# Hybrid decoder trunk on one core: the dense part keeps the written order on TensorE, ScalarE and VectorE

## The chip, the core and the metric

The kernel runs on 1 core of a Trainium2 chip. Its time is the device time of one execution in microseconds; "before" was run three times, and one more execution was profiled. Five engines work side by side, each through its own queue and in the order of that queue: TensorE (PE in the profile, its weight loads PEld), VectorE (DVE), ScalarE (ACT), GpSimd (POOL) and SyncE (SP), which here only issues the loads of the weights.

## What is computed

Two decoder layers on 256 tokens of width 1024, all in float32. A layer is a mixer and a feed-forward part, each with RMSNorm before it and a residual add after it.

```python
def _mixer(h, w_in, b_in, conv_w, conv_b, conv_ln_g, conv_ln_b, sinks, w_out, b_out):
    z = jnp.einsum('bsd,de->bse', h, w_in) + b_in
    a, gate, q, k, v = jnp.split(z, SPLITS, axis=-1)
    conv_out = _conformer_conv(a, gate, conv_w, conv_b, conv_ln_g, conv_ln_b)
    attn_out = _swa_sink_attention(q, k, v, sinks)     # reshaped to heads
    y = jnp.concatenate([conv_out, attn_out], axis=-1)
    return jnp.einsum('bse,ed->bsd', y, w_out) + b_out

for l in range(DEPTH):
    x = x + _mixer(_rmsnorm(x, attn_norm[l]), ...)
    h = _rmsnorm(x, ffn_norm[l])
    x = x + (_swiglu(h, ...) if l % 2 == 0 else _moe(h, ...))
return _rmsnorm(x, final_norm)
```

The convolution gates `a` with `sigmoid(gate)`, runs 31 causal taps over 512 channels, normalises over the channels and applies swish. The attention has 8 query heads and 2 key heads of 64, a window of 128 and a learned sink per head. The dense feed-forward (layer 0) is 1024 to 2816 and back, the other (layer 1) picks two of eight experts of width 3584 for every token.

## The kernel before

Products are made from split operands: a float32 matrix is written as a high part (`wh`, rounded by ScalarE, line 190) and a low part (`wl`, the rest, by VectorE or POOL, line 191), and three matmuls (high x high, high x low, low x high) stand for one. A piece of a weight that is split at once is a granule (`Gran`). Its raw bytes come through a ring of 7 buffers, the split parts through 4.

Everything ahead of the experts is a list of steps. `drive` (line 212) goes through it: ahead of each step it writes the conversions of the granules up to three further on, then the step itself. So the written order of an engine is the order in which these Python calls are made. The list is `mixer(0)`, `ffn(0)`, `mixer(1)`, `moe_open`. Before the change the instructions that `drive` makes aren't held to that order: a planner puts each engine's instructions in a row when the program is built, by priority and by when it expects operands and buffers to be ready. `urgent` gives some steps a higher priority there. Only the first mixer's norm and transposes are called outside of `drive`. The experts' part (`run_experts`, with `route`) is in a block with `tc.manual_schedule` already, on the same three engines.

A mixer, for channels in four blocks `c` of 128 and tokens in two tiles `t`:

- `start`: statistics (lines 268 to 270), scaled rows `h`, 16 transposes into four PSUM banks (277), and `th`/`tl`, the high and low part of the transposed rows (289, 290). Two of the eight `k` share a bank.
- 14 input projections of 24 matmuls each (353): 4 for convolution blocks 0 and 1 (`ev_g`, line 411, a sigmoid; `ev_a`, line 418, the product `up`), 4 for q, 2 for k and v, and, written after `scores`, 4 for blocks 2 and 3. Two PSUM buffers `mm` take turns.
- the taps of the convolution are VectorE operations on PSUM (425, 430). They are handed out by `conv_piece(n)`, which writes the next n taps wherever it is called: 6 with each projection, some within the softmax and PV, 12 with each output-projection step. The first 8 taps of the last block are made by TensorE (`conv_pe`, line 404), from diagonal matrices that ScalarE writes (392), and from `uh`, `ul`, the parts of `up`.
- `scores`: v is transposed (489), then six groups of score matmuls (493, 495), each followed by `softmax`: reduction (515), sink (518, 520), exponentials on ScalarE (523, 525), sum (527), reciprocal (529), and POOL's normalisation (530). Between these it calls `conv_piece`.
- `pv`: six rounds of four transposes (547), one copy (549) and the matmul with v (550).
- the output projection (578): four granules for the attention half, with the first sums of LayerNorm in between (597, 617), then `ln_out`, then four granules for the convolution half; at the end the residual adds (302).

The two lines that set the order of VectorE in a softmax, and the loop of PV:

```python
            nc.vector.tensor_tensor(den, den, es, op=ALU.add)
            nc.vector.reciprocal(den, den)
```

```python
                        pT = work.tile([P, 512], F32, name="two")
                        nc.scalar.copy(pT, pp)
                        nc.tensor.matmul(po[s * HD:(s + 1) * HD, :], v[:, kb, s * HD:(s + 1) * HD], pT,
```

The dense feed-forward has 11 rounds of gate, up and down granules (matmuls on lines 695 and 720). Behind `mixer(1)` come `route` (771 to 844), which transposes `x` and picks the experts, and the experts' 384 weight pieces (matmuls on line 910).

Of the kernel before, what the change touches and what calls it, by code (L numbers as in the profile page):

```python
# [36 lines left out]
AHEAD = 3  # L37
# [8 lines left out]
def trunk_kernel(ctx: ExitStack, tc, x_in, attn_norm, ffn_norm, w_in, b_in, conv_w, conv_b,  # L46
# [165 lines left out]
    def drive(after):  # L212

        grans = [g for g, _ in steps if g is not None] + after
        nxt = 0
        done = 0
        for g, run in steps:
            if g is not None:
                done += 1
            while nxt < len(grans) and nxt < done + AHEAD:  # L220
                grans[nxt].conv()
                nxt += 1
            if g is not None:
                run(g.h, g.l)
            else:
                run()
        steps.clear()
# [913 lines left out]
    mixer(1)  # L1141
    add(moe_open)
    grans, run_experts = expert_steps(0)
    drive(grans[:AHEAD])
    run_experts()

    def finish():
# [45 lines left out]
```

## Time and profile before

| | us |
|---|---|
| median of 3 runs | 1369.43 |
| lowest, highest | 1368.93, 1371.05 |
| profiled execution | 1375.33 |
| its span, first to last instruction | 1373.6 |
| busy in the span: PE, DVE, ACT, POOL | 1300.9, 1161.1, 1016.1, 140.8 |
| DMA read from HBM | 413.35 MB |

All times below are microseconds from the start of the profiled span. A busy PE is not a PE at its peak: the ends of matmuls are modelled, and a matmul counts as busy at either level of its clock. A row of the timeline gives start, duration, engine, line, operation, out<-in, sizes and how many were merged; in brackets stands how long the engine had been idle, and what released it. The granted clock is a share of 2.4 GHz, mean over the stretch.

### The profile page before, as it was taken

The page shows a single profiled execution, that of the slowest core. Times are in us where ns is not written, and L with a number is a line of the kernel's source. Part 1 is how long each engine was busy: PE and PEld are TensorE (multiplying, and loading weights), DVE is VectorE, ACT ScalarE, POOL GpSimd, SP SyncE. Part 2 cuts the span into 40 slices and gives each one's busy share as a digit, 9 for nine tenths or more (in the row PEclk, how much of TensorE's full clock was granted, in tenths as well). Part 3 has the DMA queues.
Part 4 walks back from the last instruction along what each step waited for, and adds up shares of the span by engine and source line. Part 5 has one row for each costly group of instructions (what it writes and reads, how often), then busy time and mean ns, then how long its engine had stood idle before and what let it go on. Part 6 is the DMA issues. An engine that isn't in the chain of part 4 may idle for free. (4 is left out here: it accounts for less than half of the span.)

```text
span 1373.6 us, 18961 instructions
## 1 busy us (share of the span) xinstructions
PE 1300.9 (95%) x6939; PEld 1132.2 (82%) x6939; DVE 1161.1 (85%) x1142; ACT 1016.1 (74%) x1110; POOL 140.8 (10%) x97
## 2 busy tenths in 40 slices
PE   6998999998989799999999999999999999999986
PEld 6866999997867687778898889888889888888874
DVE  7785555557786899999989987999999999999985
ACT  5656444445644989899888787888987988888963
POOL 5551111115450000000000000000000000000000
PEclk9899999998898999999999999999999999999998
DMA  8823565564223899999999998999999999999991
GB/s 245 252 93 93 192 193 193 190 184 123 82 96 108 312 390 382 406 406 405 406 398 386 360 362 313 365 402 406 395 401 407 366 399 394 400 406 402 407 352 49
DMA packets 150178, 416.21 MB, mean 303 GB/s; under 512 B 8599, under 2 KB 49635, under 8 KB 150049
## 3 DMA queue, kind: packets, MB, share of 16 engines
q1 hardware_dynamic: 149760, 413.38, 81.2%
q8 instruction: 89, 1.46, 0.4%
q0 software_dynamic: 288, 1.05, 0.2%
q14 instruction: 41, 0.33, 0.1%
HBM read 413.35 MB, written 1.05 MB: 302 GB/s over the span
## 5 line engine op out<-in xcount | busy, mean ns | idle before, releaser
L191 DVE TENSOR_TENSOR wl<-raw,wh 128x1792 fp32r<-128x1792 f32 (+2 forms) x460 | 848.0, 1887 | 127.0 <-ACT wh L190 125.8
L190 ACT ACTIVATE wh<-raw 128x1792 fp32r<-128x1792 f32 (+2 forms) x496 | 758.9, 1554 | 263.9 <-PE pd L910 48.0
L910 PE MATMUL pu<-wh,xg 128*128 128x448 f32 x768 | 250.6, 372 | 6.3 <-DVE h L1029 6.3
L910 PE MATMUL pg<-wh,xg 128*128 128x448 f32 x768 | 247.0, 367 | 2.4 <-ACT h L1027 2.4
L910 PE MATMUL pd<-wh,g 128*128 128x512 f32 x672 | 239.3, 397 | 6.2 <-ACT wh L190 4.1
L910 PE MATMUL pu<-wl,xg 128*128 128x448 f32 x512 | 190.2, 371 | 6.6 <-DVE wl L191 6.6
L910 PE MATMUL pg<-wl,xg 128*128 128x448 f32 x512 | 189.6, 370 | 2.4 <-DVE wl L191 2.1
L910 PE MATMUL pd<-wl,g 128*128 128x512 f32 x448 | 179.8, 401 | 3.3 <-DVE wl L191 3.3
L910 PEld LDWEIGHTS pu<-wh,xg 128*128 128x128 f32 x768 | 146.9, 191 | 18.6 <-issue 7.6
L910 PEld LDWEIGHTS pg<-wh,xg 128*128 128x128 f32 x768 | 146.2, 190 | 14.8 <-ACT h L1027 3.0
L910 PEld LDWEIGHTS pd<-wh,g 128*128 128x128 f32 x672 | 130.6, 194 | 31.7 <-ACT wh L190 5.5
L910 PEld LDWEIGHTS pu<-wl,xg 128*128 128x128 f32 x512 | 98.8, 193 | 19.6 <-DVE wl L191 12.5
L910 PEld LDWEIGHTS pg<-wl,xg 128*128 128x128 f32 x512 | 98.2, 192 | 17.6 <-DVE wl L191 9.7
L910 PEld LDWEIGHTS pd<-wl,g 128*128 128x128 f32 x448 | 86.1, 192 | 26.2 <-DVE wl L191 10.1
L430 DVE SCALAR_TENSOR_TENSOR cv<-up,wcol,cv 128x256 f32<-128x256 f32 x226 | 98.4, 487 | 5.1 <-PE cv L404 3.1
L1150 POOL DMA_DIRECT2D h<-in_final_norm_dram x1 | 0.6, 599 | 910.6 <-PE pt L1087 910.6
L191 POOL TENSOR_TENSOR wl<-raw,wh 128x1024 fp32r<-128x1024 f32 x36 | 86.2, 2408 | 38.6 <-ACT wh L190 38.3
L353 PE MATMUL mm<-th,wh 128*128 128x256 f32 x224 | 65.9, 297 | 1.1 <-ACT sg L411 1.1
L353 PE MATMUL mm<-tl,wh 128*128 128x256 f32 x224 | 65.3, 293 | 1.0 <-DVE tl L290 1.0
L353 PE MATMUL mm<-th,wl 128*128 128x256 f32 x224 | 65.3, 293 | 0.9 <-POOL wl L191 0.7
L720 PE MATMUL acc<-wh,pp 128*128 128x512 f32 x176 | 50.3, 396 | 0.0
L695 PE MATMUL cv<-tl,wh 128*128 128x256 f32 x176 | 49.2, 280 | 0.3 <-DVE tl L290 0.3
(237 smaller groups left out, 1706.5 us busy)
## 6 DMA issues: line engine op xcount, KB each, us to landing
raw<-in_moe_w_gate_dram SPq DMA_DIRECT2D x128, 896.0 KB
raw<-in_moe_w_up_dram SPq DMA_DIRECT2D x128, 896.0 KB
raw<-in_moe_w_down_dram SPq DMA_DIRECT2D x96, 1024.0 KB
raw<-in_moe_w_down_dram SPq DMA_DIRECT2D x32, 512.0 KB
raw<-in_ffn_w_gate_dram SPq DMA_DIRECT2D x11, 1024.0 KB
raw<-in_ffn_w_up_dram SPq DMA_DIRECT2D x11, 1024.0 KB
raw<-in_ffn_w_down_dram SPq DMA_DIRECT2D x11, 1024.0 KB
raw<-in_w_in_dram SPq DMA_DIRECT2D x10, 1024.0 KB
```

Source lines behind the costliest of these rows:

```text
L190: nc.scalar.activation(self.h, src, AF.Copy)
L191: (lo or lo_eng()).tensor_sub(self.l, src, f32(self.h))
L353: nc.tensor.matmul(ps[:, :S], w(a, k), b[:, k, :], start=(n == 0), stop=(n == 3 * KD - 1))
L430: nc.vector.scalar_tensor_tensor(acc, up[:, c, k:k + S], w, acc, op0=ALU.mult, op1=ALU.add)
L695: nc.tensor.matmul(ps, a[:, k, :], b[:, k, :], start=(n_ == 0), stop=(n_ == 3 * KD - 1))
L720: nc.tensor.matmul(st["o"][t][cc], a[:, kk, tk], b[:, 0, cc * 512:(cc + 1) * 512], start=(first and i == 0), stop=(last and i == 2))
L910: nc.tensor.matmul(ps, a, b, start=(first and i == 0), stop=(last and i == len(mm) - 1))
L1150: nc.gpsimd.dma_start(fg, final_norm.unsqueeze(0).to_broadcast([P, D]))
```

## The change

The call that writes all steps of the dense part is put into a `tc.manual_schedule` block for TensorE, ScalarE and VectorE. Inside it these three engines run their instructions in the order in which the Python code makes them. SP and POOL aren't named and are still ordered by the planner. No instruction, tile or buffer count is changed.

```diff
     mixer(1)
     add(moe_open)
     grans, run_experts = expert_steps(0)
-    drive(grans[:AHEAD])
+    E = mybir.EngineType
+    with tc.manual_schedule(engines={E.PE, E.Activation, E.DVE}):
+        drive(grans[:AHEAD])
     run_experts()
```

## Rows read from the trace of the kernel before

**Rows 1.** Stretches; busy us (x instructions) of PE, PEld, DVE, ACT, POOL; clock, DMA share, GB/s.

```profile
45.40:71.70 26.30, 26.30 (x144) 19.78 (x144) 18.02 (x53) 19.72 (x57) 10.96 (x10) 0.81 0.72 222
71.70:81.10 9.40, 6.83 (x44) 6.26 (x44) 7.60 (x13) 6.11 (x16) 9.22 (x4) 0.82 0.36 112
81.10:105.10 24.00, 22.23 (x88) 14.21 (x88) 19.65 (x41) 9.86 (x17) 9.76 (x5) 1.00 0.28 88
133.60:312.50 178.90, 178.88 (x1269) 166.52 (x1267) 100.94 (x99) 80.71 (x90) 19.93 (x11) 1.00 0.57 183
378.40:410.70 32.30, 29.01 (x131) 20.64 (x130) 26.86 (x53) 15.84 (x32) 18.53 (x10) 0.95 0.31 102
444.40:1373.60 929.20, 887.97 (x4323) 774.80 (x4321) 865.11 (x606) 785.94 (x701) 2.01 (x3) 0.99 0.97 372
```

**Rows 2.** DVE in order of time: start us, us, operation, xcount, idle before.

```profile
47.63 0.69 DVE L515 TENSOR_REDUCE red<-acc 128x4 f32<-128x512 f32 x1 [1.72 <-PE acc L495]
...
50.07 0.68 DVE L515 TENSOR_REDUCE red<-acc 128x4 f32<-128x512 f32 x1
...
55.74 0.15 DVE L527 TENSOR_TENSOR red<-red 128x4 f32<-128x4 f32 x1
...
56.80 0.85 DVE L527 TENSOR_TENSOR red<-red 128x4 f32<-128x4 f32 x1
...
70.10 3.12 DVE L430 SCALAR_TENSOR_TENSOR cv<-up,wcol,cv 128x256 f32<-128x256 f32 x6
```

**Rows 3.** ACT in order of time, first mixer's attention.

```profile
51.99 0.37 ACT L523 ACTIVATE pp<-acc,red 128x128 f32<-128x128 f32 x1
...
53.37 0.21 ACT L525 ACTIVATE red<-red 128x4 f32<-128x4 f32 x1
...
65.50 0.47 ACT L523 ACTIVATE pp<-acc,red 128x256 f32<-128x256 f32 x1
...
66.42 0.20 ACT L525 ACTIVATE red<-red 128x2 f32<-128x2 f32 x1
...
67.50 2.01 ACT L190 ACTIVATE wh<-raw 128x1024 fp32r<-128x1024 f32 x2
...
70.83 0.48 ACT L411 ACTIVATE sg<-mm,vcol 128x256 f32<-128x256 f32 x1
```

**Rows 4.** PE in order of time, first mixer from its last projection on.

```profile
71.75 1.91 PE L547 MATMUL acc<-ident,pp 128*128 128x128 f32 x16
...
76.62 0.58 PE L404 MATMUL cv<-ul,h 128*128 128x256 f32 x1 [2.10 <-DVE ul L231]
...
83.27 2.82 PE L550 MATMUL mm<-two,v 128*64 128x512 f32 x6 [0.17 <-ACT two L549]
...
103.96 1.15 PE L617 MATMUL mm<-h,meanm 128*128 128x256 f32 x4 [1.28 <-DVE h L610]
```

**Rows 5.** Stretches of L353 (input projection) alone: busy us (x), clock.

```profile
32.00:45.00 13.00, 13.00 (x114) 13.00 (x113) 1.00 1.07 276
```

**Rows 6.** The same of L578 (output projection) alone.

```profile
92.00:97.00 5.00, 5.00 (x23) 3.85 (x21) 1.00 0.00 2
```

**Rows 7.** ACT in order of time, one copy between PE steps.

```profile
84.38 0.59 ACT L549 COPY two<-acc 128x512 f32<-128x512 f32 x1 [0.57 <-PE mm L550]
```

**Rows 8.** POOL in order of time, first mixer.

```profile
71.57 7.23 POOL L191 TENSOR_TENSOR wl<-raw,wh 128x1024 fp32r<-128x1024 f32 x3
```

**Rows 9.** A stretch of L392 (diagonals) alone: busy us (x).

```profile
74.56:76.99 2.43, 2.43 (x9) 0.90 0.00 0
```

**Rows 10.** What L289 itself waited for: releaser, idle us of ACT, times.

```profile
  DVE tl L290: 1.4, 2
```

**Rows 11.** DVE in order of time, dense FFN's start.

```profile
127.22 2.37 DVE L290 SCALAR_TENSOR_TENSOR tl<-acc,vcol,th 128x256 fp32r<-128x256 f32 x5 [0.21 <-ACT th L289]
```

**Rows 12.** DVE in order of time, hand-over to the experts.

```profile
427.48 2.57 DVE L302 TENSOR_TENSOR x<-x,acc 128x512 f32<-128x512 f32 x4
...
429.97 2.02 DVE L191 TENSOR_TENSOR wl<-raw,wh 128x1792 fp32r<-128x1792 f32 x1
```

## What I expect, before the result

> **What bounds the kernel now.** I read four views, in this order. First the stretches [rows 1]: from 444.4 us on, the experts keep the DMA engines busy 97% of 929 us, at 372 GB/s. Nothing there is changed, and the weight ring is full when the experts begin (it stands still on the route's last steps), so the experts can't make up a late start: what the dense part loses or gains comes out at the end one for one. In the dense FFN (133.6 to 312.5) TensorE is busy 178.9 of 178.9 us; its conversions stand only a place or two from the written order and have a reserve of three granules, so I cost that stage at nothing, and if its cover went, one conversion (1.0 on ScalarE [rows 3]) would show per granule. What is left is the two mixers and the seams around them. In the first mixer VectorE works 45.3 us of the 59.7 from 45.4 to 105.1, and TensorE has gaps. Second, the orders there: the planner lets work pass other work. The second softmax group's reduction starts at 50.07, before the first group's sum at 55.74 [rows 2]; PV's sixteen transposes run at 71.75 ahead of the convolution's matmuls [rows 4]; VectorE then mixes the taps of two channel blocks. Third, what ends the mixer: the last tap of the convolution (PE waits 1.28 for h L610 at 103.96 [rows 4]). Fourth, single durations, for the sums below.
>
> **The change, part by part.** No instruction is added or taken away, and no DMA moves on its queue; SP and POOL keep the planner's order. Only who queues behind whom changes. "As written" is read from the source (functions scores, softmax, conv_pe, pv, ev_o, ln_out, start). I follow the first mixer on the time of the trace.
>
> *Softmax, one group after the other.* As written, VectorE holds each group's sum and reciprocal behind that group's exponentials, and the next group's reduction behind those. Before, scores are first reduced at 47.63 [rows 2]; as written the value transposes come first and wait for vT, an evacuation like the 0.48 of sg [rows 3] plus two transposes, some 1.1 in all: 48.8. Group 1: reduction 0.69, two taps at 0.48, two small operations at 0.15; the exponentials can start 1.25 in, take 4 x 0.35 + 0.2 [rows 3], then sum, tap, reciprocal: 3.8. Group 2: 4.0, with one copy more in ScalarE's way. Groups 3 to 5 have no taps left: 0.69 + 0.15, two exponentials and the sink's 1.1 (65.50 to 66.42 and 0.2 [rows 3]), sum and reciprocal 0.3, some 0.2 between engines: 2.45; and 0.4 where POOL's normalisation of the group before holds a small VectorE operation up (L527 took 0.85 instead of 0.15 [rows 2]): 2.85 each. Group 6 to its last exponential: 2.45. So 48.8 + 3.8 + 4.0 + 8.55 + 2.45 = 67.6. Behind it in ScalarE's queue stand one conversion (1.0), the table load that ends at 70.83 today (1.3) and the sigmoid of projection 10 (0.48 [rows 3]): 70.4. Projections 10 and 11 fit in front of that; 12 needs the bank which this sigmoid frees. 12 and 13 are 48 matmuls at 0.114 [rows 5], 5.6: the last projection ends at 76.1 instead of 71.75, +4.4.
>
> *Convolution on TensorE.* Before, five diagonals and the weight's rounding lay in front of it. As written VectorE first does twelve taps of one block, 12 x 0.52 = 6.2 from 70.9 [rows 2], then up (0.5): 77.7; uh 0.45; then ul, which today takes 2.1 while POOL works (PE waits 2.10 for it [rows 4], POOL 3 x 2.41 [rows 8]). POOL's four roundings would be done about 78.7, so I take 79.2 for ul, wtl right behind, then fifteen diagonals at 0.3 (eight new ones in 2.43 [rows 9]): matmuls end at 84.5, against 81.1: +3.4. With ul and wtl held up as today it is 87.0; with a free POOL 84.0. Meanwhile VectorE's next tap waits for these matmuls, and all taps queue behind it.
>
> *PV.* As written each of six rounds is four transposes (0.48 [rows 4]), ScalarE's copy (0.59 [rows 7]), two matmuls (six took 2.82 with their waits [rows 4]; two of this width take 0.46 without [rows 6]), and nothing fills the waits. The trace has no such round alone: from 1.8 (0.48 + 0.59 + 0.46 + 0.25 between engines) to 2.7 (TensorE's share at half the clock). I take 2.2, since neither level has a row: 13.2, to 97.7.
>
> *After PV* TensorE has 48 output-projection matmuls and 20 of the LayerNorm sums (two in the trace for each in the source) before the point at 105.1. At 0.23 (21 to 22 in 5.00 [rows 6]) that is 15.6: 113.5 with a little waiting. VectorE's 42 taps (31 and 23 less the twelve) from 84.5 at 0.52 at most, two splits and four LayerNorm operations end by 111.3, so they are covered; TensorE becomes the end of this stage. First mixer: 113.5 - 105.1 = +8.4 (bounds +5.3 with PV at 1.8 and a free POOL, +15.4 with PV at 2.7, the slow ul and 1.7 for first matmuls behind PV at half the clock). The second mixer's part behind the projections takes 32.3 today against 33.4 [rows 1], and would take the same as the first: +9.5 (+6.4 to +16.5).
>
> *Seams.* The FFN's start: th of an odd k reads the bank that tl of the even k before it still reads, and ScalarE waits for VectorE there [rows 10]. Today the banks alternate; at the pace of the last five tl (2.37 [rows 11]) eight take 3.8. As written a pair takes th, tl, th in a row, 3 x 0.48 + 0.1: four pairs 6.2, and a last tl, 6.7. That is 2.9 more; the statistics, which the planner had put between, come after it, and the third projection waits for them: some 0.4, in all 3.3 (2 to 6). The second mixer has the same pairs, but waits for a sigmoid anyway: +0.7 (0 to 1.5). Hand-over: today four residual adds (2.57) run at 427.48 and the third expert conversion's VectorE half (2.02) behind them [rows 12]; as written it goes first, and the router's transposes wait: +2.4 (2.0 to 2.9). The last granule of each output projection is now converted after LayerNorm's ScalarE work: +0.7 twice (0 to 2.8 in all).
>
> *Sum.* 8.4 + 9.5 + 3.3 + 0.7 + 2.4 + 1.4 = 25.7. The profiled execution took 1375.33, of which 1373.6 is its span; it would become 1401.0. The median of the runs is 1369.43, 5.9 lower; on it the sum gives 1395.1. All low ends together give +15.7 (1385), all high ends +45 (1414).
>
> **The rivals.** *The waits are absorbed (1377).* VectorE idles 8.3 + 1.8 + 4.4 = 14.4 us in the first mixer [rows 1]; if delays of TensorE vanished in that, only the seams' 7.8 would remain. Against it: 68 matmuls stand behind PV, and no VectorE idle time shortens them. *VectorE decides in both orders (1363, faster).* Its work between 45.4 and 105.1 is 45.3 us; if the written places of the taps let it run through, with half of the 14.4 saved per mixer, 2 x 7.2 less the seams' 7.8 is 6.6 faster. It decides once PV is over by 105.1 - 7.2 - 15.6 = 82.3; against it, the taps as written wait for the very matmuls that end at 84.5. *The lower clock (1409).* The granted clock is 0.82 in the stretch where TensorE waits for uh and ul, with half of 2.4 GHz in part of it, and 1.00 in the busier one behind it [rows 1]. Spread over PV and the first output projection, the 1.2 GHz level costs 6 x 0.45 in PV and some 4 behind it, 7 per mixer, 14 on top of my sum. [...] *The change doesn't bind (1369)*: the planner still moves work inside the block, and the order stays.
>
> **How the numbers follow.** My forecast, 1385 to 1409 around 1395, has 0.60; absorbed 0.13; lower clock 0.12; faster 0.09; not binding 0.06. The range 1372 to 1412 leaves out the faster and unbound cases and the end of the clock case. About 0.2% (2.7 us) is what a measurement of this kernel can tell from no change: faster 0.09, same 0.06, slower 0.85.
>
> **What would show it.** In the profile after: each softmax reduction (L515) behind the reciprocal before it, and a last sigmoid near 70; projections ending near 76; L547 and L550 alternating six times with ScalarE's L549 between; TensorE, not VectorE's L610, ahead of the last L617, near 113; the last residual add of the first layer behind a conversion; FFN and experts unchanged in length. I am wrong if PV ends before 90, if the experts' stretch changes by more than 3 us, or if reductions still overtake exponentials.

## The result, and the profile after

The changed kernel takes 1410.55 us (median of three, 1405.64 to 1412.08) against 1369.43: it is slower, 1.0292 times as long (95% interval 1.0268 to 1.0317). In the run e1_again below, beside new executions of the kernel before, it took 1408.98 against 1369.33 (1.0297, 1.0266 to 1.0327). Its profiled execution took 1405.64 with a span of 1403.6, so the two traces differ by 30.0, the two medians by some 40; the last part of the explanation comes back to that.

The same stretches after the change, cut at the ends of the same work (10th and 14th projection, last L404, last L550, last L617), then the FFN, PV of the second mixer, the hand-over and the experts; columns as in [rows 1]. Projections are counted from 1 from here on, so those of blocks 2 and 3 are the 11th to the 14th; the prediction counted the same four from 0, as 10 to 13.

```profile
46.45:77.90 31.45, 30.75 (x147) 21.47 (x146) 19.79 (x55) 16.33 (x50) 14.65 (x10) 0.73 0.56 176
77.90:85.87 7.97, 5.25 (x27) 4.78 (x27) 2.46 (x5) 5.44 (x18) 2.61 (x2) 0.79 0.45 139
85.87:99.95 14.08, 9.81 (x38) 3.52 (x35) 10.19 (x25) 4.11 (x7) 0.00 (x0) 1.00 0.00 0
99.95:117.08 17.13, 15.98 (x69) 12.59 (x68) 10.85 (x23) 6.63 (x11) 9.59 (x4) 1.00 0.39 124
138.41:327.86 189.45, 188.32 (x1323) 173.92 (x1322) 109.77 (x108) 87.95 (x108) 15.36 (x13) 1.00 0.56 179
407.01:421.08 14.07, 9.80 (x37) 3.51 (x35) 10.19 (x25) 4.11 (x7) 0.00 (x0) 1.00 0.00 1
455.43:475.55 20.12, 14.95 (x109) 13.27 (x108) 13.46 (x34) 4.22 (x11) 0.69 (x1) 0.83 0.45 162
475.55:1403.57 928.02, 887.64 (x4323) 774.86 (x4321) 864.64 (x606) 785.13 (x701) 2.02 (x3) 0.99 0.97 373
```

From the 10th to the 14th projection it now takes 31.45 us (26.5 before), with TensorE busy 30.75 of them at a clock of 0.73. PV is a stretch of its own, 14.1 us, at full clock; 17.1 us of output projection and LayerNorm sums follow. The stages of the two mixers differ by 0.4 us at most. The experts are as long as before (928.0; 929.2 in [rows 1]): what the dense part lost is in the end.

VectorE in order of time, first mixer (start, duration, operation; in brackets how long it had been idle and what released it), against [rows 2]:

```profile
61.12 0.67 DVE L515 TENSOR_REDUCE red<-acc 128x2 f32<-128x512 f32 x1
...
63.64 0.16 DVE L527 TENSOR_TENSOR red<-red 128x2 f32<-128x2 f32 x1 [1.04 <-ACT red L525]
...
63.84 0.17 DVE L529 RECIPROCAL red<-red 128x2 f32<-128x2 f32 x1
...
63.92 0.67 DVE L515 TENSOR_REDUCE red<-acc 128x2 f32<-128x512 f32 x1
...
85.91 4.80 DVE L430 SCALAR_TENSOR_TENSOR cv<-up,wcol,cv 128x256 f32<-128x256 f32 x12 [5.01 <-PE cv L404]
...
100.62 0.69 DVE L231 TENSOR_TENSOR tl<-mm,th 128x512 fp32r<-128x512 f32 x1 [4.17 <-ACT th L230]
...
101.23 7.54 DVE L430 SCALAR_TENSOR_TENSOR cv<-up,wcol,cv 128x256 f32<-128x256 f32 x18
...
108.67 2.17 DVE L608 TENSOR_TENSOR h<-h,sg 128x256 f32<-128x256 f32 x2
...
111.10 0.47 DVE L610 SCALAR_TENSOR_TENSOR h<-cv,vcol,sg 128x256 f32<-128x256 f32 x1
```

Now each reduction (L515) stands behind the reciprocal (L529) of the group before, 2.80 apart (61.12, 63.92). The taps behind `conv_pe` wait 5.01 for L404, and those behind PV's last half 4.17.

The two subtractions that are merged in the L608 row above, with the shortest, median and longest duration in ns, and what POOL did at that time:

```profile
L608 DVE TENSOR_TENSOR h<-h,sg x2: 411/1124/1837, 108.7 to 110.4; 128x256 f32<-128x256 f32 x2
```

```profile
107.85 2.38 POOL L191 TENSOR_TENSOR wl<-raw,wh 128x1024 fp32r<-128x1024 f32 x1 [0.18 <-ACT wh L190]
```

The first L608 started under a rounding of POOL and took 1.84; the second started behind it and took 0.41.

TensorE in PV and behind it, against [rows 4]; ScalarE's first sigmoid of blocks 2 and 3, against [rows 3]:

```profile
86.98 1.07 PE L550 MATMUL mm<-two,v 128*64 128x512 f32 x2 [0.68 <-ACT two L549]
...
87.99 0.66 PE L547 MATMUL acc<-ident,pp 128*128 128x128 f32 x4
...
89.32 1.07 PE L550 MATMUL mm<-two,v 128*64 128x512 f32 x2 [0.67 <-ACT two L549]
...
110.57 1.78 PE L617 MATMUL mm<-h,meanm 128*128 128x256 f32 x7 [1.15 <-DVE h L608]
...
115.19 1.89 PE L617 MATMUL mm<-h,meanm 128*128 128x256 f32 x8
```

```profile
70.15 1.28 ACT L411 ACT_TABLE_LOAD   x1
71.45 0.47 ACT L411 ACTIVATE sg<-mm,vcol 128x256 f32<-128x256 f32 x1
```

A PV round is four transposes, 0.7 of waiting for ScalarE's copy, two matmuls, and nothing in between: six times 2.35. The sigmoid of the 11th projection ended at 71.92 and TensorE the 12th projection at 71.84: the 13th needs both, a bank and TensorE.

The hand-over to the experts, VectorE and TensorE, against [rows 12], and what L289 waited for in the whole kernel, against [rows 10]:

```profile
451.66 6.62 DVE L191 TENSOR_TENSOR wl<-raw,wh 128x1792 fp32r<-128x1792 f32 x3 [2.11 <-ACT wh L190]
458.21 2.47 DVE L302 TENSOR_TENSOR x<-x,acc 128x512 f32<-128x512 f32 x4
```

```profile
460.14 1.15 PE L771 MATMUL pg<-ident,x 128*128 128x128 f32 x5 [4.71 <-DVE x L302]
```

```profile
  DVE tl L290: 4.6, 8
```

Three conversions in a row now stand ahead of the residual adds, and the router's transposes wait 4.71 for these adds. ScalarE's th waits for VectorE's tl eight times (two before).

Lengths of the stages in all fourteen traces, in us, from the ends of the named matmuls (first / second mixer; FFN from the last L578 of the first mixer to the last L720; hand-over from the last L578 of the second to the first L910):

| trace | 10th to 14th projection | to last L404 | PV, to last L550 | to last L617 | FFN | hand-over | span |
|---|---|---|---|---|---|---|---|
| before | 26.5 / 26.1 | 9.2 / 9.4 | 6.9 / 6.9 | 17.1 / 15.8 | 189.1 | 15.1 | 1373.6 |
| b_again | 21.9 / 26.1 | 7.8 / 9.4 | 6.9 / 6.9 | 17.1 / 15.8 | 189.1 | 15.1 | 1370.4 |
| after | 31.4 / 31.5 | 8.0 / 7.6 | 14.1 / 14.1 | 17.1 / 17.1 | 193.5 | 20.1 | 1403.6 |
| e1_again | 31.4 / 31.4 | 8.7 / 7.9 | 14.2 / 14.1 | 17.1 / 17.1 | 192.5 | 20.3 | 1405.7 |
| e2_pv | 31.4 / 31.4 | 8.6 / 8.0 | 10.0 / 10.1 | 17.1 / 17.1 | 192.8 | 19.6 | 1399.4 |
| e3_softmax | 32.5 / 31.0 | 8.2 / 8.1 | 14.3 / 14.1 | 17.1 / 17.1 | 192.8 | 20.3 | 1407.2 |
| e5_mix | 34.7 / 34.7 | 6.9 / 7.0 | 14.1 / 14.1 | 17.1 / 17.1 | 193.0 | 20.4 | 1410.8 |
| e9_both | 27.9 / 28.1 | 7.7 / 7.5 | 14.1 / 14.1 | 17.1 / 17.1 | 193.5 | 20.2 | 1395.9 |
| e4_seams | 31.4 / 31.5 | 8.4 / 7.6 | 14.1 / 14.1 | 17.1 / 17.1 | 190.8 | 16.6 | 1398.1 |
| e6_pe | 33.3 / 33.2 | 8.3 / 8.4 | 14.1 / 14.1 | 15.7 / 15.7 | 190.3 | 15.1 | 1398.1 |
| e7_actdve | 32.5 / 32.7 | 7.0 / 7.1 | 7.1 / 7.0 | 17.6 / 17.6 | 193.0 | 20.6 | 1391.0 |
| e8_all | 35.1 / 35.4 | 4.6 / 4.6 | 7.9 / 7.9 | 18.3 / 17.4 | 191.9 | 20.9 | 1392.0 |
| e10_best | 28.0 / 28.0 | 10.4 / 8.1 | 7.4 / 7.0 | 18.9 / 20.7 | 189.2 | 16.2 | 1384.4 |
| e11_pv_first | 26.9 / 28.0 | 9.1 / 9.1 | 3.6 / 3.6 | 21.4 / 22.4 | 189.2 | 15.1 | 1381.4 |

The columns "to last L404" and "PV" don't hold the same work in every row. Where the planner orders TensorE (before, b_again, e7_actdve), and in e8_all and e10_best, the first sixteen of PV's transposes stand ahead of `conv_pe`'s matmuls (1.91 us in [rows 4]); in e11_pv_first all transposes and two whole rounds do. There the two columns are to be read as a sum.

### The profile page after: what moved, and what is told of

It reads as the page before. It is cut to its first block, busy times and chain, and to the rows that moved or that the text cites. A ratio compares the mean times of both kernels' runs of the same rounds, so it can differ in the third digit from the quotient of the medians.

```text
span 1403.6 us, 18957 instructions
## 1 busy us (share of the span) xinstructions
PE 1316.0 (94%) x6939; PEld 1136.8 (81%) x6939; DVE 1159.2 (83%) x1142; ACT 1012.9 (72%) x1106; POOL 134.6 (10%) x97
## 3 DMA queue, kind: packets, MB, share of 16 engines
q0 software_dynamic: 288, 1.05, 0.2%
HBM read 413.35 MB, written 1.05 MB: 295 GB/s over the span
## 5 line engine op out<-in xcount | busy, mean ns | idle before, releaser
L910 PE MATMUL pu<-wh,xg 128*128 128x448 f32 x768 | 249.5, 371 | 5.5 <-DVE h L1029 5.5
L910 PE MATMUL pg<-wh,xg 128*128 128x448 f32 x768 | 247.8, 368 | 2.4 <-ACT h L1027 2.4
L910 PE MATMUL pd<-wh,g 128*128 128x512 f32 x672 | 239.3, 397 | 6.2 <-ACT wh L190 4.1
L910 PE MATMUL pu<-wl,xg 128*128 128x448 f32 x512 | 189.2, 370 | 6.7 <-DVE wl L191 6.6
L910 PE MATMUL pg<-wl,xg 128*128 128x448 f32 x512 | 190.3, 372 | 2.2 <-DVE wl L191 1.9
L910 PE MATMUL pd<-wl,g 128*128 128x512 f32 x448 | 179.8, 401 | 3.2 <-DVE wl L191 3.2
L910 PEld LDWEIGHTS pu<-wh,xg 128*128 128x128 f32 x768 | 146.3, 191 | 17.5 <-issue 6.7
L910 PEld LDWEIGHTS pg<-wh,xg 128*128 128x128 f32 x768 | 146.8, 191 | 14.9 <-ACT h L1027 3.0
L910 PEld LDWEIGHTS pd<-wh,g 128*128 128x128 f32 x672 | 130.6, 194 | 31.6 <-ACT wh L190 5.5
L910 PEld LDWEIGHTS pu<-wl,xg 128*128 128x128 f32 x512 | 98.1, 192 | 19.4 <-DVE wl L191 12.5
L910 PEld LDWEIGHTS pg<-wl,xg 128*128 128x128 f32 x512 | 98.8, 193 | 17.0 <-DVE wl L191 9.2
L910 PEld LDWEIGHTS pd<-wl,g 128*128 128x128 f32 x448 | 86.3, 193 | 26.2 <-DVE wl L191 10.0
L430 DVE SCALAR_TENSOR_TENSOR cv<-up,wcol,cv 128x256 f32<-128x256 f32 x226 | 96.2, 485 | 12.1 <-PE cv L404 10.0
L353 PE MATMUL mm<-th,wh 128*128 128x256 f32 x224 | 66.6, 297 | 0.8 <-ACT th L289 0.4
L353 PE MATMUL mm<-tl,wh 128*128 128x256 f32 x224 | 66.0, 295 | 1.2 <-DVE tl L290 1.1
L353 PE MATMUL mm<-th,wl 128*128 128x256 f32 x224 | 65.1, 291 | 0.0
L720 PE MATMUL acc<-wh,pp 128*128 128x512 f32 x176 | 50.3, 396 | 0.0
```

The costliest lines, as they stand in the source:

```text
L353: nc.tensor.matmul(ps[:, :S], w(a, k), b[:, k, :], start=(n == 0), stop=(n == 3 * KD - 1))
L430: nc.vector.scalar_tensor_tensor(acc, up[:, c, k:k + S], w, acc, op0=ALU.mult, op1=ALU.add)
L720: nc.tensor.matmul(st["o"][t][cc], a[:, kk, tk], b[:, 0, cc * 512:(cc + 1) * 512], start=(first and i == 0), stop=(last and i == 2))
L910: nc.tensor.matmul(ps, a, b, start=(first and i == 0), stop=(last and i == len(mm) - 1))
```

## The experiments

Ratios are to executions of the kernel before in the same batch. The changed kernel is meant where an edit is described, unless another is named.

**The changed kernel again.** Nothing is edited.

> The changed kernel once more, nothing edited. Its three timed runs were 1405.64, 1410.55 and 1412.08 with mean granted clocks of 0.969, 0.967 and 0.965, against 1369.43 before; the trace (span 1403.6 against 1373.6) accounts for 30 us. Theory A (the order alone costs the 30 us of the trace, the rest is TensorE's clock, which differs from run to run): times spread over 1403 to 1413, longer where the clock is lower, stages of equal clock as long as in the first trace. Theory B (the cost is the same in every run, and the first trace was only short by chance somewhere): times within 1409 to 1413 and a trace whose mixers are longer at an unchanged clock.

1408.98 (1407.76 to 1410.55), at clocks of 0.969 to 0.965; the times alone don't tell A from B. The stages of the table do: they are those of the first trace but for 1.0 us at most (the experts, not in the table, took 2.3 longer). Against the first trace of the kernel before, the two are 30 and 32 us longer. And one thing was new: TensorE regained its clock 3 us sooner in the first score block, ended the 12th projection at 68.85, and then waited for the sigmoid, so that the four projections took 31.4 us again.

**PV one round ahead.** In outline:

```diff
+ pend = [turn_(0)]            # four transposes of round 0
  for r in rounds:
-     transposes(r)
-     copy(r)
+     copy(pend.pop())
+     pend.append(turn_(r + 1))
      matmul(r)
```

> In the written order the four transposes of the next PV round stand ahead of the matmul of this one, in both mixers; everything else as in the changed kernel. Theory A (TensorE and ScalarE waiting for each other is what makes PV 14.1 us long, and TensorE is what ends the mixer behind it): a round falls from 2.35 to transposes plus matmul, 0.66 + 1.07 = 1.73, PV to 10.9, and the kernel is 6 us shorter than the changed one (3.2 per mixer). Rival B (VectorE's taps end the mixer anyway, since the square sums of LayerNorm wait for line 608): PV shorter, but the last LayerNorm matmul no earlier, 0 to 1 us in the total.

1400.06 (1398.35 to 1401.49), 8.9 less than e1_again. TensorE, the same two rounds:

```profile
87.88 0.66 PE L545 MATMUL acc<-ident,pp 128*128 128x128 f32 x4
...
88.47 1.07 PE L561 MATMUL mm<-two,v 128*64 128x512 f32 x2
...
89.47 0.66 PE L545 MATMUL acc<-ident,pp 128*128 128x128 f32 x4
...
93.89 1.93 PE L561 MATMUL mm<-two,v 128*64 128x512 f32 x4
```

The second pair starts without a wait (88.47), the last two pairs run in one. PV fell from 14.1 to 10.0 in both mixers and the stage behind it stayed at 17.1, so all that follows came earlier by as much: theory A, with 4.0 per mixer instead of 3.2.

**Softmax tails behind the next group.** In outline:

```diff
  reduction(g); exponentials(g)
- sum(g); reciprocal(g); normalise(g)
+ if g > 0:
+     sum(g - 1); reciprocal(g - 1); normalise(g - 1)
```

> In the written order each softmax group's sum, reciprocal and normalisation stand behind the next group's reduction and exponentials. Theory A (the groups one behind the other hold the sigmoid of projection 10 and with it the projections): groups come 1.9 to 2.2 us apart instead of 2.8, the last exponential ends 3 to 4 us earlier, the sigmoid follows projection 11 (ended 69.0) at once instead of at 71.9, and the kernel is 4 to 5 us shorter (2.4 per mixer). Rival B (TensorE at half its clock in the score matmuls, 0.73 in this stretch, is what sets it: they end at 64.5 either way): softmax shorter, projections end as late as before the edit, 0 to 1 us.

1407.34 (1405.56 to 1409.26): 1.6 less, which the spread of the two doesn't tell apart. The last exponential did come earlier, 20.7 and 20.0 us behind the 10th projection instead of 22.7 in both mixers, and the sigmoid stood ready behind its table load:

```profile
66.46 1.28 ACT L411 ACT_TABLE_LOAD   x1
68.82 0.48 ACT L411 ACTIVATE sg<-mm,vcol 128x256 f32<-128x256 f32 x1 [1.08 <-PE mm L353]
```

It now waits for TensorE (mm L353), not the other way round. The four projections took 32.5 and 31.0 us. Rival B: TensorE itself holds them.

**The 11th projection between the score groups.** First the granted clock of the score block, in stretches of 4 us (length, busy us of PE and instructions, clock, DMA share, GB/s): the changed kernel, the kernel before in its first trace and in a second one (b_again), and this edit.

```profile
50.00:54.00 4.00, 4.00 (x14) 0.60 1.00 375
54.00:58.00 4.00, 4.00 (x10) 0.50 1.08 354
58.00:62.00 4.00, 4.00 (x10) 0.50 0.59 187
62.00:66.00 4.00, 4.00 (x12) 0.50 0.00 0
66.00:70.00 4.00, 4.00 (x29) 0.77 0.01 4
```

```profile
50.00:54.00 4.00, 4.00 (x9) 0.50 1.00 383
54.00:58.00 4.00, 4.00 (x18) 0.50 1.08 352
```

```profile
50.00:54.00 4.00, 4.00 (x23) 1.00 0.99 235
54.00:58.00 4.00, 4.00 (x20) 1.00 1.03 385
```

```profile
50.00:54.00 4.00, 4.00 (x15) 0.50 1.00 375
54.00:58.00 4.00, 4.00 (x24) 0.67 1.08 356
58.00:62.00 4.00, 4.00 (x16) 1.00 0.63 202
```

```diff
  scores of groups 0, 1
+ 11th projection (24 matmuls)
  scores of groups 2 to 5
- 11th projection
  sigmoid of the 11th projection
```

> In the written order the 24 matmuls of projection 11 stand between the second and the third score group, its sigmoid where it was; the rest as in the changed kernel. Theory A (the 48 score matmuls in one block let TensorE's granted clock fall to 0.5 for 14 to 17 us, where the order before had 10): the stretch at 0.5 gets shorter by 4 to 7 us, the 14th projection ends 27 to 29 us after the 10th instead of 31.4, and the kernel is 4 to 8 us shorter than the changed one. Rival B (the softmax chain and the sigmoid hold the projections): they still end 31 us after the 10th, 0 us; more, if the sigmoid now comes later.

1412.61 (1410.77 to 1412.89), nothing gained. The clock did return sooner, as theory A said (1.00 from 58 on instead of 0.50 up to 66), and the 12th projection ended at 67.4. But then TensorE stood still:

```profile
73.57 0.58 PE L353 MATMUL mm<-th,wh 128*128 128x256 f32 x1 [6.19 <-ACT sg L411]
```

6.19 us for the sigmoid behind the softmax chain. The four projections took 34.7. So two holds of nearly equal length lie on the same stretch, and e3_softmax and e5_mix each took away one.

**Both at once.** The edits of e3_softmax and e5_mix together.

> Softmax tails behind the next group and projection 11 between the score groups, both at once, nothing else edited. Theory A (two limits of the same length hold the projections in the written order, the clock of the score block and the sigmoid behind the softmax chain, so that taking one away moved nothing): with both gone the 14th projection ends 25 to 28 us after the 10th instead of 31.4, and the kernel is 6 to 12 us shorter than the changed one. Rival B (a third thing holds it, such as the sigmoid's table load or a conversion ahead of it): again 30 us or more, 0 to 3 us in the total.

1400.13 (1398.00 to 1402.17), 1.0208 times before (1.0187 to 1.0229): 8.9 less than e1_again, 12 by the two ratios. The projections took 27.9 and 28.1 us instead of 31.4: theory A. Neither edit alone had shortened the time.

**The seams.**

```diff
- banks[k // 2][:, k % 2]        # transposed rows, two neighbouring k in a bank
+ banks[k % 4][:, k // 4]
- while nxt < done + AHEAD: convert          # ahead of every step
+ while nxt < done + AHEAD and step not in (last ev_o, residual, ffn start): convert
```

> Two edits of the seams: the transposed rows of neighbouring k lie in different PSUM banks (k modulo 4 instead of k // 2), so that th of one k and tl of the k before it never meet in a bank; and the conversions that were written ahead of the last output-projection step stand behind the residual adds (and behind the FFN's start). Theory A: th and tl of the FFN take 3.8 to 4.2 us instead of 6.3 (2.3 less), the second mixer's 0.8 less, and the hand-over to the experts 4.5 less, as the adds no longer wait for three conversions (6.6 us of VectorE): 7 to 8 us shorter. Rival B (the conversions are only moved: the experts' first matmuls wait for the third one instead): the hand-over gives back 0 to 1 us, the total is 3 us shorter.

1401.74 (1400.22 to 1402.78), 7.2 less. No th waited for a tl any more (eight times, 4.6 us, before the edit), and the first FFN projection took 3.8 us instead of 6.3. Of these 2.5, about 1.0 was given back, since the conversion moved behind the FFN's start came late there (the first row below; the third projection took 4.1 instead of 3.1). The hand-over fell from 20.1 to 16.6, though the router still waited 2.10 for adds that stood behind two conversions (the second row).

```profile
145.34 0.39 PE L701 MATMUL mm<-th,wl 128*128 128x256 f32 x1 [0.75 <-DVE wl L191]
...
453.33 0.66 PE L777 MATMUL pg<-ident,x 128*128 128x128 f32 x4 [2.10 <-DVE x L303]
```

The Trainium skill, "PSUM — Partial Sum Buffer", section "PSUM bank collisions raise a hardware error ⚠️", says that two engines must be kept off one bank (in the same partitions) by semaphores, whatever the columns. The waits of th for tl fit that: the two read different columns of one bank, and the waits vanished when neighbouring k got different banks. What a collision itself does, no run here shows.

**One engine's order at a time.**

```diff
- with tc.manual_schedule(engines={E.PE, E.Activation, E.DVE}):
+ with tc.manual_schedule(engines={E.PE}):                     # e6_pe
+ with tc.manual_schedule(engines={E.Activation, E.DVE}):      # e7_actdve
```

> Only TensorE keeps the written order; ScalarE and VectorE are planned as before. Theory A (what costs is TensorE's own order: scores in a block, PV's rounds behind the convolution): 1390 to 1403, that is 20 to 33 of the 40 us. Rival B (VectorE's and ScalarE's order cost: softmax groups, seams, conversions ahead of the adds): 1370 to 1385.

> ScalarE and VectorE keep the written order, TensorE is planned. Theory A: what is left of the cost is the seams (the hand-over's 5, the FFN's start 3, the second mixer's start 1) and some of the mixers: 1375 to 1388. Rival B: 1395 to 1409, as in the changed kernel.

TensorE alone: 1402.63 (1400.19 to 1405.17), 31.4 above before. ScalarE and VectorE alone: 1393.38 (1392.08 to 1395.39), 22.2 above, between the two ranges that I had given. Together they cost 40, not 53.6, and the table shows why. PV belongs to TensorE's order (with the column before it 22.4 under that order, 14.1 without), hand-over and most of the FFN's start to the others' (20.6 and 193.0 against 15.1 and 190.3). But the projections take 33 us with either alone: each order brings a hold of its own there, and two holds side by side cost as much as one.

**Everything, three times.** e8_all has all edits, the sixteen diagonals written right behind the scores, PV's first four rounds of transposes ahead of `conv_pe`, and eight taps of block 2 while TensorE works on block 3. e10_best moves what stood in the way: half of the diagonals behind each of the last two sigmoids, the FFN's statistics ahead of its transposes, only the residual ahead of the last conversions. e11_pv_first also does PV's first two rounds whole ahead of `conv_pe`.

> The written order with all edits at once: softmax tails behind the next group, projection 11 between the score groups, the diagonals written behind the scores, four rounds of PV's transposes ahead of the convolution's matmuls and the others one round ahead, eight taps of block 2 ahead of the taps that wait for TensorE, the seams' two edits. If the single costs add up (PV 9 or more, seams 7, clock 4 to 8, convolution ahead of PV and taps 6 to 10), it takes 1370 to 1385. If an order written by hand can do what the planner's did and more at the seams, 1360 to 1370; if the costs overlap, so that one takes the place of another, 1385 to 1395.

1393.52 (1392.12 to 1394.51): the costs overlapped. The sixteen diagonals (4.9 us of ScalarE) now stood ahead of the sigmoid, and projections took 35.

> The written order with all edits, mended where they stood in each other's way: half of the diagonals behind each of the last two sigmoids instead of ahead of them, only the residual (not the FFN's start) ahead of the last conversions, the FFN's statistics ahead of its transposes, the first PV half split behind the next copy, one conversion more ahead of ln_out. If the costs found so far are all there is: the 14th projection 26 us after the 10th, the first mixer's last LayerNorm matmul at 104 to 107, the FFN's first round as long as before, 1366 to 1378. If not, 1380 to 1392, and the stage that is still longer than before shows which.

1384.78 (1384.49 to 1386.50), 1.0091 times before (1.0072 to 1.0110). FFN and hand-over were within 1.2 of before, projections at 28.0, but behind PV 18.9 and 20.7: the mixers stayed longer.

> The order of e10_best, with PV's first two rounds whole (copies and matmuls, too) ahead of the convolution's matmuls, and LayerNorm's first sums behind the last attention half of the output projection. In e10_best TensorE waits 3 us for uh and ul in the first mixer, and 0.7 for line 608's subtractions. If these waits are what its mixers are longer by, behind the projections, it gets 2 to 3 us shorter per mixer, 1378 to 1381. If VectorE's taps set the end there, nothing moves: 1384 to 1386, with TensorE's waits moved to the LayerNorm sums. That it comes below the kernel before (1372) would need 13 us, more than these waits hold.

1382.66 (1380.22 to 1383.45), 1.0090 (1.0068 to 1.0111). That is 2.1 less than e10_best, but its kernel before was 2.0 faster too (1369.79, 1371.81), so the ratio is the same, and the times don't show a gain. In the traces the first mixer got 2.5 shorter behind the projections and the second 0.7, where I had given 2 to 3 for each, since most of the wait only moved; TensorE behind PV:

```profile
90.43 0.73 PE L623 MATMUL acc<-wh,tl 128*128 128x512 f32 x2 [3.87 <-DVE tl L235]
```

It waits 3.87 for VectorE, whose queue holds taps ahead of that split. So with e10_best's order about two thirds of the 40 us (all but 13) are undone, but no order tried here reached the planner's.

**The kernel before again.**

> The kernel before once more, nothing edited, for its trace. Its runs lie between 1365 and 1377 us, with granted clocks from 0.982 down to 0.973. If the clock makes the spread, a trace at 0.976 or more shows stretches at half the clock that are missing or shorter than in the first trace (0.973), and the stages without such a stretch as long as there.

One execution, 1372.15, span 1370.4, clock 0.974, so not the higher clock that I had asked for; yet one of the stretches was missing. In the first score block the clock never fell (1.00 from 50 to 58, where the first trace had 0.50), for the same instructions in the same order. The projections took 21.9 us instead of 26.5, and the first mixer 53.7 from its 10th projection to its last L617 instead of 59.7; the second mixer was the same to 0.1. Half of the 6 us came back in the experts (932.1 instead of 929.2), whose length lies between 928.0 and 932.4 in these fourteen traces, for a reason that I haven't found.

## Why the prediction was right, and where not

The direction held, the mechanism in the main, and the time lay in the range; the forecast of 1395 was 15 us short. That 1410.55 is still inside is partly luck: the range ended at 1412, and the longest of the three executions (1412.08) was past it. Of the 15, 4.6 lie in the traces (30.3 between the profiled executions against 25.7), as a sum of misses of both signs, and the rest is between traces and medians.

- *Softmax to last projection, +4.4*: measured +5.0 and +5.4. The chain of groups came as worked out (2.80 apart against 2.85, sigmoid at 71.9 against 70.4). The step failed in its cause, though: I had let projections 10 and 11 fit in front of that at full clock. TensorE went through the score block at half of 2.4 GHz (0.50 from 54 to 66) and was itself ready for the 13th only at 71.84. Either alone gives the delay, as e3_softmax, e5_mix and e9_both show, so that +4.4 came near is partly luck.
- *Convolution, matmuls ending at 84.5*: 85.87, the 1.4 late with the sigmoid. The part itself took 8.0, as forecast (8.4), and less than the 9.2 before only because those held sixteen of PV's transposes as well.
- *PV, 13.2*: 14.1 in both mixers, and 10.0 once the wait was filled (e2_pv). The mis-sized term is the pair of matmuls: I took 0.46 from the output projection's, two of the same width [rows 6], and a pair took 1.07. PV's are slower, 0.43 each (four take 1.93 and two 1.07 in e2_pv), as six in 2.82 [rows 4] had already said; that row should have been the lower bound too.
- *After PV, 15.6, VectorE covered*: 17.1. VectorE's last tap and LayerNorm operation ended where I put them (111.57 against 111.3), but TensorE doesn't only need the last: the sums of blocks 0 and 1 need L608. In VectorE's queue L608 stands behind all those taps, and in TensorE's queue the sums stand ahead of the last attention granule. TensorE waits 1.15 for it, with 28 matmuls still to go. Most of that wait comes from POOL: TensorE was there at 109.42, and two L608 of 0.41 would have ended at about 109.5 (an estimate from the rows above), but the first took 1.84 under POOL's rounding. That is read from the rows; no run took the rounding away. Cover has to be checked for each consumer, not for the end of the stage.
- *The mixers together, +17.9*: +11.0 and +12.0 from the 10th projection to the last L617. Another 1.0 lay ahead of the first mixer's 10th projection; the second trace doesn't have it.
- *FFN start, +3.3*: +4.5 and +3.5 in the two traces, with the residual adds, which now wait for a conversion. *Second mixer's start, +0.7*: +0.1 and +0.4. *Late granules, +1.4*: from the last L617 to the last L578 it took 17.3 and 17.2 us (18.1 and 17.2 in the second trace) instead of 18.3 and 18.6, so it cost nothing.
- *Hand-over, +2.4*: +5.0. I saw the third conversion ahead of the adds, and not that the two before it slide as well: by the planner they had ended 1.8 ahead of the last output matmul, as written they end 0.8 behind it (451.66 + 6.62 - 2.02, against 455.43). With conversions moved behind the adds (e10_best) it is +1.1, with TensorE's order alone (e6_pe) 0.
- *Experts, 0*: -1.2 in the first trace, +1.2 in the second. "One for one" holds only to some 3 us: b_again's experts took 2.9 longer than those of the first trace.

Of the rivals, "not binding" fell with the order of VectorE, "absorbed" and "VectorE decides" with the stages; e11_pv_first, where TensorE waits for the taps, shows that VectorE is close behind all the same. The lower clock gave nearly the right time (1409) by the wrong place: PV's rounds ran at 1.00 in both mixers, and the clock fell in the score block, where TensorE was busy. The Trainium skill, "TensorE: Matmul & The Clock Gate", section "HAM oscillation — how this bites in real kernels", puts a return of the throttle down to waits between bursts of matmuls, in its case waits for a DMA that are several times as long as PV's 0.7. PV at 1.00 therefore doesn't speak against it. The stage that ends with the last L404 fits it (TensorE busy 5.25 of 7.97, clock 0.79); the fall in the score block is of another kind, since TensorE had no wait there.

What stays open: the medians lie 40 apart, the traces 30 (first pair) to 35 (the second traces of both). The kernel before was timed at granted clocks of 0.973 to 0.982, 1377.12 to 1364.96 us, and both its traces were at the low end (0.973 and 0.974); the changed one at 0.965 to 0.969. So the changed kernel keeps less of its clock; that is measured. b_again shows one place where the kernel before gains some of it in some executions, while both traces of the changed kernel have 0.50 in that block. Time and clock go together: a straight line through the 28 executions of the kernel before that were timed beside the experiments falls by 1.05 us for each 0.001 of clock, and the seven of the changed one give 1.04. The middle clocks (0.977 and 0.967) lie 0.010 apart, those of the traces 0.004 and 0.005; by that line (an estimate) this goes with 5 to 6 of the 5 to 10 us. Where the clock fell in these executions isn't known, as they left no trace.

## What to carry to other kernels

A written order isn't free of cost when it was written for a planner: a loop of "transpose, copy, multiply" that a planner pulls apart becomes a ping-pong between two engines, and work written early "to be ahead" stands ahead of something urgent. Where an edit to one of two queues changes nothing, look for a second hold of the same length before dropping the theory; take both away at once. When you write off a stage as covered, follow each consumer into its queue, not the end of the covering work.

## What the runs showed of the hardware

- TensorE's granted clock fell to half of 2.4 GHz while the engine was busy without a gap (4.00 of 4.00 us): in the block of score matmuls, 64 rows deep, each pair behind a mask matmul. It rose again while projections (128 rows) ran, and stayed up in PV, where TensorE was busy 9.8 of 14.1 us. It also fell in the stage that ends with the last L404 (mean 0.79), where TensorE was busy 5.25 of 7.97 us.
- The same instructions in the same order had that fall in one trace of the kernel before and not in another (0.50 and 1.00 from 50 to 58 us): 4.6 us between two executions of one program.
- Matmuls of 512 columns took 0.43 us each in PV (plain float32 operands, 64 columns of weights) and 0.23 in the output projection (rounded operands, 128 columns of weights; [rows 6]), both at full clock. The operands make the difference, not the columns of weights: the LayerNorm sums (plain float32, 128 columns of weights, 256 columns) took some 0.22 each (eight in 1.89), the input projections (rounded, 128 and 256 as well) 0.114 [rows 5].
- VectorE's subtraction L608 (both operands in SBUF, 256 columns) took 1.84 us while POOL rounded a weight, and 0.41 behind that, in both mixers and both traces of the changed kernel. The taps (L430, one operand in PSUM) were hardly held up: 12 in 4.80 us with POOL idle, 18 in 7.54 with POOL rounding most of the time.
